# An encoder trunk on one core: the output product takes all 1536 rows in its seven block products, and the fourth weight sum grows in the second's tile

## The chip, the cores and the metric

The kernel runs on one core of one Trainium2 chip. The metric is device microseconds of one execution, given as a median of several runs. Profiles are of one execution. The engines are TensorE (PE, with PEld for its weight loads), VectorE (DVE), ScalarE (ACT), GpSimd (POOL) and SyncE (SP). Each executes its own instructions in program order; semaphores order them against one another.

## The reference

A trunk of two layers on 512 tokens of width 1024, in float32. Each layer normalises its input, projects it (mixer heads, memory query heads, gate), runs eight mixer heads and four heads of cross attention into 256 memory tokens, multiplies the 1536 concatenated head outputs by a SiLU gate, and multiplies by `w_out` onto the residual.

```python
for i in range(DEPTH):                      # 2 layers
    h = rmsnorm(x, norm_g[i])
    mem_h = rmsnorm(mem, mem_norm_g[i])
    ...                                     # layer 0: dilated window attention, layer 1: axial rotary GQA
    o_mem = memory_attention(q_mem, mem_h, w_mem_kv[i], mem_qn_g[i], mem_kn_g[i])
    y = jnp.concatenate([o_mix, o_mem], axis=-1) * jax.nn.silu(gate)   # (1, 512, 1536)
    x = x + jnp.einsum('bse,ed->bsd', y, w_out[i])                     # (1536, 1024)
```

## The kernel before

**Precision.** Every large product is made of three matmuls: both operands are split into a high part (a cast to `float32r`) and a low part (the rest), and high x high, low x high and high x low are accumulated. `mm_early` (L170, L171) issues the two that need the weights' high part, `mm_late` (L174) the one that needs their low part.

**Block products.** Most products are done as 2 x 2 blocks with seven block products instead of eight (Winograd's form of Strassen's method): `s_chunk` goes through `PRODUCTS`. The left factor comes as seven blocks (`12`, `11`, `S1`, `S2`, `S4`, `S3`, `22`), sums and differences of quarters. The right factor's seven blocks come from `Weights`: four quarters from DRAM and the sums `T1 = 12 + 11`, `T2 = T1 + 22` and so on, with signs laid out beforehand. Each finished product is copied (`keep`) or added onto an earlier one (`add`) out of PSUM, and each output block is handed to a consumer `ev`.

**Weights.** An item of weights is a tile of 128 x 1024. It is loaded by SP (L246), possibly summed (`sum`: T1 on DVE at L264 or, from layer B on, by an accumulating DMA from POOL at L260; T2 by a tile-to-tile accumulating DMA, L269; T3 by one from DRAM, L274; T4 by a tile-to-tile one in the tile of block `21`, L279), then split: high part on ACT (L295), low part on DVE (L305), in rings of four. `Weights.advance()` is called once behind every group of matmuls. It issues, in this order, low parts, one sum, high parts and loads; `LEAD` and `ripe` demand a number of groups between a load or sum and what uses it. `KEEP` bounds the raw tiles alive, and `PLAN` lists the chunks: `W2` and `W2b` have two items per block, `W1` and `W1b` one, `T2` and `O1` are plain products.

**Order of the work.** One program order is written out by the host: matmul groups of the projections in sequence, and behind each group `drv.tick()`, in which generators issue their next step: evictions, norms, attention heads (`attn_a` in layer A, `attn_b` in layer B, both "bulk" generators), gates and so on. A generator that waits for another's result yields slots. So attention is spread between the groups of later projections, and a step's place in the order decides what covers it. Where a group needs a block that no generator has made yet, `drv.tick()` is called without a matmul group until it exists.

**The end of a layer.** The gate is projected in three chunks of four heads: memory heads (8 to 11), heads 0 to 3, heads 4 to 7. `gates` multiplies each output block by the heads' output (stored to DRAM by the attention, `od`, and loaded back as `og`). The first two chunks (1024 rows of the product) are turned into seven blocks by `prep_y`. The output product `out_proj` runs `s_chunk` on these 1024 rows: 7 products x 2 items, 14 groups of 12 matmuls of 512 columns. Each output block is added by an accumulating DMA (L876) onto a tile `acc` that was loaded with the residual. The other 512 rows, heads 4 to 7, are the direct part: `gates` splits them into `ys` (L801, L803), and `out_rest` multiplies them plainly, 2 column halves x 4 token blocks, 8 groups of 12 matmuls, added to `acc` by DVE at L756. In layer A the result goes on through norm and transposition into the second layer's first chunks, behind eight groups of the memory projection (`T2b`); in layer B it is written out.

Of the kernel before, what the change touches and what calls it, by code (L numbers as in the profile page):

```python
# [34 lines left out]
PLAN = ["W2"] + ["T2"] * 2 + ["W1", "W2s"] + ["W2" if c.isdigit() else "W1" for c in A_ORDER[1:]] + ["W2"] + ["O1"] * 2 + ["T2b"] * 2 + ["W1bs"] + ["W1b"] * 6 + ["W2b"] + ["O1"] * 2  # L35
# [90 lines left out]
def trunk_kernel(ctx: ExitStack, tc: tile.TileContext, x, mem, wall, norm_g, mem_norm_g, gcol,  # L126
# [57 lines left out]
    GROUPS = {"T2": (2, 2), "T2b": (2, 2), "O1": (1, 4)}  # L184

    def pieces(kind):

        return 2 * GROUPS[kind][0] if kind in GROUPS else 4 if kind in ("W1", "W1b", "W1bs") else 8

    class Weights:  # L190
        def __init__(self):
# [3 lines left out]
            for c in SEQ:  # L195
# [13 lines left out]
                else:  # L209
                    n = 1 if kind in ("W1", "W1b", "W1bs") else 2  # L210
                    at = {k: d + i * n for i, k in enumerate(("21", "11", "12", "22"))}
                    self.allocs += [((c, k, x), at[q] + x, kind) for k, q in LOADS for x in range(n)]
                    for k in ORDER:
                        for x in range(n):
                            self.items.append((c, k, x))
                            self.last.append(g)
                            self.need.append(len(self.items))
                            if k[0] == "T":
                                self.sums.append(((c, k, x), at["11" if k == "T1" else "22"] + x))
# [10 lines left out]
        def use(self, key):  # L230
            if key[1] == "T4":
                key = (key[0], "21", key[2])
# [18 lines left out]
        def sum(self, force=False, want=None):  # L251

            for n, (key, d) in enumerate(self.sums[:8]):
# [110 lines left out]
    def s_chunk(n, act, ev, tokens=True, pre=None, half=False, soon=False):  # L364
# [20 lines left out]
        def add(q, name, u, b):  # L385
# [3 lines left out]
            V.tensor_tensor(t, b, t, ALU.subtract if q == "12" else ALU.add)  # L389
# [4 lines left out]
        for i, (a, s, fresh) in enumerate(PRODUCTS):  # L394
            while a not in act:
                drv.tick()
            if fresh:
                bank[s] = [pj() for _ in range(units)]
            for x in range(units):
                wh, wo = [t.rearrange("p (k c) -> p k c", c=n) for t in W.take()]  # L400
                ah, al = act[a][:, 0], act[a][:, 1]
                def regions():
                    for b in range(2):
                        o = bank[s][b] if units == 2 else bank[s][0][:, b * 256:(b + 1) * 256]
                        for k in range(per):
                            yield b, k, x * per + k, slice(b * 128, (b + 1) * 128), o

                for b, k, kk, bs, o in regions():
# [4 lines left out]
                    st = fresh and kk == 0 and (units == 2 or b == 0)  # L413
# [4 lines left out]
                for b, k, kk, bs, o in regions():  # L418
                    if tokens:
                        mm_late(o, ah[:, kk, bs], wo[:, k], kk == 3)  # L420
                    else:
                        mm_late(o, wo[:, k, bs], ah[:, kk], kk == 3)
                drv.free()
                W.advance()
                if x == units - 1:
# [317 lines left out]
    def out_rest(ys, acc, done, evac):  # L743

        for n in range(2):
            def group(w, u, b, p):
                cs = slice(b * 128, (b + 1) * 128)
                while any(y is None for y in ys):
                    drv.tick()
                for k in range(4):  # L750
                    mm_early(p, ys[k][0][:, cs], w[k][0], ys[k][0][:, cs], w[k][1], k == 0)
                for k in range(4):
                    mm_late(p, ys[k][1][:, cs], w[k][0], k == 3)

            def ev(b, p, n=n):
                V.tensor_tensor(acc[b][n], p, acc[b][n], ALU.add)  # L756
                yield 1
                while (n, b) not in done:
                    yield 1
                yield from evac(n, b, acc[b])  # L760
            chunk(1, 4, group, ev)


    def gates(od, o_done):

        ys, yf, y_done, YW = [None] * 4, [None, None], set(), {}

        def gate(H, first, g, half=False):


            yt = [[m4(F32R, "y").rearrange("p (h t) -> p h t", h=2) for _ in range(2)] for _ in range(2)] if g == 2 else None
# [3 lines left out]
            def ev(q, u, t):  # L775
# [23 lines left out]
                yield 1  # L799
                tv = t.rearrange("p (h t) -> p h t", h=2)  # L800
                A.copy(yt[j][0][:, :, ts], tv)  # L801
                yield 1
                V.tensor_tensor(yt[j][1][:, :, ts], tv, yt[j][0][:, :, ts].bitcast(F32), ALU.subtract)  # L803
                y_done.add((g, i, j))
                if {(2, 0, j), (2, 1, j)} <= y_done:
                    for k in range(2):
                        ys[2 * j + k] = (yt[j][0][:, k], yt[j][1][:, k])
# [51 lines left out]
        return gate, prep_y, YW, ys  # L859

    def out_proj(YW, ys, src, evac, tiles, half=False):

        acc, done = {}, set()

        def load():
# [709 lines left out]
```

## Time and profile before

| | |
|---|---|
| median of 3 runs | 966.77 us (965.88 to 971.68) |
| profiled execution | 968.3 us, its span 966.5 us |
| PE busy | 946.8 us, 98% of the span, 5682 matmuls |
| DVE, ACT, POOL busy | 791.4, 681.7, 341.4 us |
| output product in layer A, first group to the group behind it | 572.83 to 644.09 us |
| output product in layer B, first group to the end of the span | 882.94 to 966.5 us |
| DMA | 209.81 MB, 217 GB/s on average |
| mean granted clock of TensorE | 0.996 |

Times in the rows are microseconds from the start of the span; a row names the engine, the line of the kernel, the operation, and the tiles written and read. Matmul durations in the rows overlap; the distance between starts tells the rate. A bracket at the end gives the idle time of the engine just before, and what ended it.

### The profile page before, as it was taken

The page shows a single profiled execution, that of the slowest core. Times are in us where ns is not written, and L with a number is a line of the kernel's source. Part 1 is how long each engine was busy: PE and PEld are TensorE (multiplying, and loading weights), DVE is VectorE, ACT ScalarE, POOL GpSimd, SP SyncE. Part 2 cuts the span into 40 slices and gives each one's busy share as a digit, 9 for nine tenths or more (in the row PEclk, how much of TensorE's full clock was granted, in tenths as well). Part 3 has the DMA queues.
Part 4 walks back from the last instruction along what each step waited for, and adds up shares of the span by engine and source line. Part 5 has one row for each costly group of instructions (what it writes and reads, how often), then busy time and mean ns, then how long its engine had stood idle before and what let it go on. Part 6 is the DMA issues. An engine that isn't in the chain of part 4 may idle for free.

```text
span 966.5 us, 16604 instructions
## 1 busy us (share of the span) xinstructions
PE 946.8 (98%) x5682; PEld 833.2 (86%) x5682; DVE 791.4 (82%) x1411; ACT 681.7 (71%) x1701; POOL 341.4 (35%) x482
## 2 busy tenths in 40 slices
PE   8999999999999999999999999999899999999998
PEld 5879888888888888888899997788899999998886
DVE  5898676878888888888888999769878898769883
ACT  5775689686868686868685657546768977879770
POOL 1512423557554545454726011322332330111010
PEclk9999999999999999999999999999899999999999
DMA  9989956969686868685959889889766687777744
GB/s 360 317 235 327 271 116 172 294 120 268 149 258 143 262 150 258 154 261 132 283 132 241 266 206 297 268 242 366 167 157 129 199 235 179 207 204 190 206 131 131
DMA packets 89129, 209.81 MB, mean 217 GB/s; under 512 B 25298, under 2 KB 36050, under 8 KB 89044
## 3 DMA queue, kind: packets, MB, share of 16 engines
q1 hardware_dynamic: 69892, 145.76, 43.4%
q0 software_dynamic: 17856, 60.83, 33.4%
q10 hardware_dynamic: 1296, 2.16, 0.6%
q8 instruction: 45, 0.74, 0.3%
q14 instruction: 40, 0.33, 0.1%
HBM read 157.27 MB, written 12.65 MB: 176 GB/s over the span
## 4 chain that ended last, share of the span: by engine, by line
PE 80%; DVE 8%; DMA 6%; ACT 3%; issue 2%; POOL 1%; SPq 0%; DVEq 0%; POOLq 0%; ACTq 0%
PE pj L170 21%; PE pj L171 21%; PE pj L174 20%; DVE wo L305 2%; PE qT L585 2%; PE sa L1106 1%; PE oo L1208 1%; PE pt L1187 1%; PE sa L1102 1%; PE ptb L1405 1%; DMA og<-odb 1%; DMA acc<-sn 1%; DMA wl<-wl 1%; DMA grB<-in_qn_b_dram 1%; DMA od<-o 1%
## 5 line engine op out<-in xcount | busy, mean ns | idle before, releaser
L305 DVE TENSOR_TENSOR wo<-wl,wh 128x1024 fp32r<-128x1024 f32 x255 | 315.1, 1242 | 6.0 <-ACT wh L295 5.8
L295 ACT CAST wh<-wl 128x1024 fp32r<-128x1024 f32 x255 | 268.5, 1060 | 29.3 <-PE pj L171 18.9
L170 PE MATMUL pj<-wh,hS 128*128 128x512 f32 (+1 forms) x448 | 159.0, 368 | 3.9 <-DVE sn L389 3.9
L171 PE MATMUL pj<-wh,hS 128*128 128x512 f32 (+1 forms) x448 | 153.6, 356 | 0.0
L170 PE MATMUL pj<-wh,h 128*128 128x512 f32 (+1 forms) x336 | 117.9, 365 | 0.0
L171 PE MATMUL pj<-wh,h 128*128 128x512 f32 (+1 forms) x336 | 114.0, 353 | 0.0
L437 POOL TENSOR_TENSOR rstd<-mse,half 128x4 f32<-128x4 f32 (+2 forms) x98 | 103.1, 1052 | 8.2
L174 PE MATMUL pj<-wo,hS 128*128 128x512 f32 (+1 forms) x448 | 100.8, 355 | 2.0 <-DVE wo L305 2.0
L170 PEld LDWEIGHTS pj<-wh,hS 128*128 128x128 f32 x448 | 85.9, 192 | 14.8 <-issue 2.6
L171 PEld LDWEIGHTS pj<-wh,hS 128*128 128x128 f32 x448 | 86.1, 192 | 10.3
L372 ACT COPY sn<-pj 128x512 f32<-128x512 f32 x132 | 73.1, 590 | 29.7 <-PE pj L174 29.7
L436 POOL TENSOR_SCALAR mse<-hss 128x4 f32<-128x4 f32 (+1 forms) x86 | 45.1, 525 | 132.2 <-ACT junk L573 128.0
L174 PEld LDWEIGHTS pj<-wo,hS 128*128 128x128 f32 x448 | 75.3, 191 | 14.5 <-DVE wo L305 2.7
L573 ACT ACTIVATE junk<-sn 128x128 f32<-128x128 f32 x264 | 79.1, 308 | 4.1 <-DVE sn L383 4.1
L1050 POOL TENSOR_TENSOR ta<-sn,tabs 128x128 f32<-128x128 f32 (+1 forms) x64 | 37.4, 592 | 118.6 <-DVE sn L578 92.0
L389 DVE TENSOR_TENSOR sn<-pj,sn 128x512 f32<-128x512 f32 x99 | 67.7, 686 | 12.3 <-PE pj L174 11.8
L174 PE MATMUL pj<-wo,h 128*128 128x512 f32 (+1 forms) x336 | 74.8, 352 | 0.0
L171 PEld LDWEIGHTS pj<-wh,h 128*128 128x128 f32 x336 | 63.8, 190 | 7.4
L170 PEld LDWEIGHTS pj<-wh,h 128*128 128x128 f32 x336 | 63.6, 189 | 7.4 <-DVE sn L389 0.2
L279 POOL DMA_DIRECT2D wl<-wl x33 | 29.1, 881 | 111.9 <-DVE wo L305 56.0
L174 PEld LDWEIGHTS pj<-wo,h 128*128 128x128 f32 x336 | 56.0, 189 | 8.7
L578 DVE TENSOR_TENSOR sn<-sn,rstd 128x512 f32<-128x512 f32 (+1 forms) x82 | 48.0, 594 | 7.2 <-POOL rstd L437 7.2
(235 smaller groups left out, 2335.1 us busy)
## 6 DMA issues: line engine op xcount, KB each, us to landing
wl<-in_wall_dram SPq DMA_DIRECT2D x222, 512.0 KB, 7.0
wl<-wl POOLq DMA_DIRECT2D x66, 512.0 KB, 5.5
wl<-in_wall_dram POOLq DMA_DIRECT2D x42, 512.0 KB, 8.5
acc<-sn POOLq DMA_DIRECT2D x16, 256.0 KB, 4.8
od<-o SPq DMA_DIRECT2D x12, 256.0 KB, 5.6
og<-od SPq DMA_DIRECT2D x12, 256.0 KB, 5.5
odb<-o SPq DMA_DIRECT2D x12, 256.0 KB, 3.4
og<-odb SPq DMA_DIRECT2D x12, 256.0 KB, 4.2
```

Source lines behind the costliest of these rows:

```text
L170: T.matmul(o, a, b, start=start, stop=False, skip_group_check=True)
L171: T.matmul(o, c, d, start=False, stop=False, skip_group_check=True)
L174: T.matmul(o, a, b, start=False, stop=stop, skip_group_check=True)
L295: A.copy(wh, self.tile[self.items[i]])
L305: V.tensor_tensor(wo, self.tile[key], wh.bitcast(F32), ALU.subtract)
L372: A.copy(t, b)
L389: V.tensor_tensor(t, b, t, ALU.subtract if q == "12" else ALU.add)
L436: G.tensor_scalar(e, ss, EPS, None, ALU.add)
L437: G.tensor_tensor(r, e, half[:, 0:n], ALU.pow)
L573: A.activation(jk, p[:, j * 128:(j + 1) * 128], AF.Square, scale=QS, accum_out=ss[:, j:j + 1])
L578: V.tensor_tensor(xn[:, 0:n], p.rearrange("p (a b) -> p a b", a=4)[:, 0:n], r[:, 0:n, None].to_broadcast([128, n, 128]), ALU.mult)
L1050: G.tensor_tensor(ta[:, 0:n], xn[:, 0:n, 0:32], ropeA[:, 0, b, s0:s0 + n], ALU.mult)
```

## The change

`out_rest` and the direct part go. Every block product of the output product now takes 768 of the 1536 rows instead of 512: three items and three groups per product (kinds `W3` and `W3b`), 21 groups in all. The first two groups of a product use the blocks of `prep_y` (`YW`), the third uses blocks (`YL`) that a new generator, `prep_l`, makes from the gate's last chunk in the same seven combinations. `gates` therefore stops splitting that chunk and keeps its four blocks in `yl`. A loop in `s_chunk` ticks until the block that the coming group needs exists; it stood ahead of each product and now stands ahead of each group.

The residual is no longer held in `acc`: for three of the four output quarters an accumulating DMA adds it onto a kept product (`Base.add`), for the fourth DVE adds the product onto a loaded tile (`Base.tile`). The consumers `ev_o` and `ev_o2` get each output block once, final.

The fourth weight sum, in all chunks: T4 is now made in T2's tile, by adding the block `21` from DRAM, once T2's own low part is done; before, it was made in block `21`'s tile by adding T2's tile.

```diff
-PLAN = [...] + ["W2"] + ["O1"] * 2 + ["T2b"] * 2 + ["W1bs"] + ["W1b"] * 6 + ["W2b"] + ["O1"] * 2
+PLAN = [...] + ["W3"] + ["T2b"] * 2 + ["W1bs"] + ["W1b"] * 6 + ["W3b"]
-T1_DMA = 17
+T1_DMA = 16
-KEEP = {"T2": 8, "T2b": 6, "O1": 6, "W1": 9, "W2": 10, "W2s": 9, "W1bs": 9, "W1b": 7, "W2b": 9}
+KEEP = {"T2": 8, "T2b": 6, "W3": 11, "W3b": 9, "W1": 9, "W2": 10, "W2s": 9, "W1bs": 9, "W1b": 7}
...
                             if k != "T4":
-                                self.users[c, k, x] = 1 if k in ("22", "T3") or k == "11" and c >= T1_DMA else 2
+                                self.users[c, k, x] = 1 if k in ("21", "22", "T3") or k == "11" and c >= T1_DMA else 2
...
-                    if not (self.ripe(self.lo_at, (c, "21", x), force, 1) and self.ripe(self.at, (c, "T2", x), force)):
+                    if not self.ripe(self.lo_at, (c, "T2", x), force, 1):
                         continue
-                    self.tile[key] = self.tile[c, "21", x]
-                    G.dma_start(self.tile[key], self.tile[c, "T2", x], accum_op=ALU.add)
-                    self.use((c, "T2", x))
+                    self.tile[key] = self.tile[c, "T2", x]
+                    G.dma_start(self.tile[key], wall[d], accum_op=ALU.add)
...
         def keep(name, u, b):
+            if base and name == "s3":
+                t = snap[name, u] = base.tile(u)
+                V.tensor_tensor(t, b, t, ALU.add)
+                c = snap[u, "22"] = snap["s5", u]
+                V.tensor_tensor(c, c, b, ALU.subtract)
+                yield 1
+                yield from ev("22", u, c)
+                return
             t = snap[name, u] = s2(name="sn")
-            A.copy(t, b)
+            A.activation(t, b, AF.Copy, scale=-1.0 if base and name == "s2" else 1.0)
             yield 1
+            if base:
+                base.add(name, u, t)
...
         for i, (a, s, fresh) in enumerate(PRODUCTS):
-            while a not in act:
-                drv.tick()
             if fresh:
                 bank[s] = [pj() for _ in range(units)]
-            for x in range(units):
+            groups = units if more is None else 3
+            for x in range(groups):
                 wh, wo = [t.rearrange("p (k c) -> p k c", c=n) for t in W.take()]
-                ah, al = act[a][:, 0], act[a][:, 1]
+                src = act if x < units else more
+                while a not in src:
+                    drv.tick()
+                ah, al = src[a][:, 0], src[a][:, 1]
...
-                V.tensor_tensor(t, t, o, ALU.mult)
-                yield 1
-                tv = t.rearrange("p (h t) -> p h t", h=2)
-                A.copy(yt[j][0][:, :, ts], tv)
-                yield 1
-                V.tensor_tensor(yt[j][1][:, :, ts], tv, yt[j][0][:, :, ts].bitcast(F32), ALU.subtract)
+                V.tensor_tensor(t, t, o, ALU.mult)
+                yl[i, j] = t
...
+        def prep_l():
+            def put(k, src):
+                t = m4(F32R, "yl")
+                A.copy(t[:, 0:512], src)
+                V.tensor_tensor(t[:, 512:1024], src, t[:, 0:512].bitcast(F32), ALU.subtract)
+                YL[k] = t.rearrange("p (a k t) -> p a k t", a=2, k=2)
...
+            yield from wait((0, 0))
+            put("11", yl[0, 0])
+            yield from wait((0, 1))
+            put("12", yl[0, 1])
+            yield from wait((1, 1), (1, 0))
...
+            put("S1", s1)               # then S2, S4, S3 and 22, a sum ahead of each
...
+    class Base:
...
+        def add(self, name, u, t):
+            G.dma_start(t, self.part(*{"z": (0, 0), "s2": (0, 1), "s5": (1, 1)}[name], u), accum_op=ALU.add)
...
-        drv.spawn(load(), ACC_AT)
-        s_chunk(512, YW, ev, half=half)
-        out_rest(ys, acc, done, evac)
+        drv.spawn(base.load(), ACC_AT)
+        s_chunk(512, YW, ev, half=half, more=YL, base=base)
```

More of the change, by code (lines that the diff above doesn't have):

```diff
@@ L741, in mem_attn @@
                             (0, top, 1), (1, recip, 1), (3, hi, 1), (3, lo, 1), (4, out_, 1), step=step)
[L743 to L756, printed above, removed]
-                yield 1
-                while (n, b) not in done:
-                    yield 1
-                yield from evac(n, b, acc[b])
-            chunk(1, 4, group, ev)
     def gates(od, o_done):
-        ys, yf, y_done, YW = [None] * 4, [None, None], set(), {}
+        yf, yl, y_done, YW, YL = [None, None], {}, set(), {}, {}
         def gate(H, first, g, half=False):
-            yt = [[m4(F32R, "y").rearrange("p (h t) -> p h t", h=2) for _ in range(2)] for _ in range(2)] if g == 2 else None
             if g < 2:
```

142 lines of the change are left out of this document (83 added, 59 removed).

## The prediction

> **What bounds the kernel now.** I read the page first, then the instructions in order of time around the two output products, one engine at a time, then groups and windows of those stretches.
>
> ```profile
> span 966.5 us, 16604 instructions
> PE 946.8 (98%) x5682; PEld 833.2 (86%) x5682; DVE 791.4 (82%) x1411; ACT 681.7 (71%) x1701; POOL 341.4 (35%) x482
> PE 80%; DVE 8%; DMA 6%; ACT 3%; issue 2%; POOL 1%; SPq 0%; DVEq 0%; POOLq 0%; ACTq 0%
> ```
>
> TensorE (PE) is busy almost always and makes up 80% of the chain that ended last. A change pays by the PE instructions it takes out, and costs wherever PE, which executes in program order, meets an instruction whose data are late. Today the output product covers the end of each layer's attention. Layer A (start, duration, engine, line):
>
> ```profile
> 575.58 0.39 PE L170 MATMUL pj<-wh,y 128*128 128x512 f32 x1
> 578.30 0.39 PE L170 MATMUL pj<-wh,y 128*128 128x512 f32 x1
> 644.09 0.39 PE L170 MATMUL pj<-wh,act 128*128 128x512 f32 x1
> ...
> 577.06 1.29 DVE L843 TENSOR_TENSOR ys<-ys,yf 128x512 f32<-128x512 f32 x2
> 579.46 0.16 DVE L1149 TENSOR_TENSOR nmM<-stp,oth 128x8 f32<-128x8 f32 x1
> 608.18 0.69 DVE L1220 TENSOR_TENSOR o<-oo,o 128x512 f32<-128x512 f32 x1 [1.30 <-PE oo L166]
> 618.25 1.38 DVE L798 TENSOR_TENSOR sn<-sn,og 128x512 f32<-128x512 f32 x2 [1.84 <-DMA og<-od]
> ```
>
> The first two rows start the second and third groups of the output product; a group is 12 matmuls of 512 columns: 2.72 us, 0.227 us a matmul. The third row starts the first group behind the product's 22. When the third group starts, the last head has not yet combined its softmax sums (nmM, 579.46); its output is complete at 608.87, and stored, reloaded and gated at 619.6. PE runs block products meanwhile, because the last part of the gated heads, `ys`, is first read in `out_rest`. Layer B is alike:
>
> ```profile
> 882.94 0.48 PE L170 MATMUL pj<-wh,y 128*128 128x512 f32 x1
> 891.13 0.39 PE L164 MATMUL sb<-kbT,qb 128*128 128x512 f32 x1
> 931.98 0.64 PE L174 MATMUL ob<-pbT,vb 128*128 128x256 f32 x4
> 933.05 0.33 SPq L1295 DMA_DIRECT2D odb<-o  x1
> 937.72 1.37 DVE L798 TENSOR_TENSOR sn<-sn,og 128x512 f32<-128x512 f32 x2 [2.48 <-DMA og<-odb]
> 961.50 1.07 PE L174 MATMUL pj<-wh,y 128*128 128x512 f32 x4
> ```
>
> Its product starts at 882.94; the attention steps behind the second group run from 891.13 to 932.6, spread between groups; the gated values exist at 939.1. The last matmul ends at 962.57, 3.9 us before the span does.
>
> **The change part by part.** *Matmuls.* Per layer `out_rest` loses 2 x 4 x 12 = 96; the seven products gain 7 x 12 = 84. That is 12 x 0.227 = 2.7 us less per layer, 5.4 in all; 21 groups stand where 22 stood.
>
> *The moved need.* Each product now has three groups, the third on `YL`, which `prep_l` makes from the gate's last block. Its first reader is the third group of the first product, on `YL["12"]`, and that needs the last heads of the layer. While it is missing, `s_chunk` calls `drv.tick()` with no matmuls between. The compared instruction orders show it: in layer A all of the last head's remaining PE work (16 transposes, 8 and 12 matmuls) stands between the second and the third group, where before it was spread behind groups 6 to 10; in layer B ten attention steps stand there, where before they stood one by one. This term decides: what was covered is in the open, with store, reload, gating and splitting behind it. Behind the waiting matmul stand all 19 later groups; on the other engines only the evictions of the first product wait for it. On SP the gap holds the last loads of gate and residual but no weight loads, since `W.advance()` runs by groups; so the sums on POOL keep their lead in groups.
>
> Layer A, from 578.4 (end of the second group). VectorE (DVE) has done L843 at 578.3 before; one more first weight sum (1.2 us) and one split less put it at about 580.0 after gating. From there to the last head's combine it has 37 instructions in order: 20 that are 512 wide (block sums and low parts of y, gating, splits), one weight low part, 8 scalings, 8 small ones.
>
> ```profile
> L305 DVE TENSOR_TENSOR wo<-wl,wh 128x1024 fp32r<-128x1024 f32 x15 | 18.3, 1223 | 1.7 <-ACT wh L295 1.7
> L823 DVE TENSOR_TENSOR yS<-yf,yS 128x512 fp32r<-128x512 f32 x4 | 2.6, 690 | 0.0
> L1174 DVE TENSOR_SCALAR p<-p,c 128x256 f32<-128x256 f32 x6 | 1.8, 351 | 0.0
> 608.90 0.33 SPq L1002 DMA_DIRECT2D od<-o  x1
> ```
>
> Back to back they overlap by 0.09: 20 x 0.60 + 1.13 + 8 x 0.27 + about 1.2 = 16.5 us. Waits for ScalarE's high parts and PE's 12 matmuls add some 2.7 and the combine 0.6: 599.8. Store to gating took 618.25 - 608.90 = 9.35; both multiplies 1.3 and the low part 0.7 make it 611.2, where PE goes on. Bounds: 604 (no waits, and 937.72 - 933.05 = 4.7 from store to gating as in layer B), and 621 (every step at its old pace: 619.6 + 1.4).
>
> *The clock after a gap.*
>
> ```profile
> 685.25 0.55 PE L170 MATMUL pj<-wh,hS 128*128 128x256 f32 x1 [2.47 <-DVE sn L389]
> 690.34 0.28 PE L170 MATMUL pj<-wh,hS 128*128 128x256 f32 x1
> 693.22 0.28 PE L170 MATMUL pj<-wh,hS 128*128 128x256 f32 x1
> ...
> 686.00:688.00 2.00, 2.00 (x12) 2.00 (x11) 2.00 (x4) 1.20 (x9) 0.70 (x1) 0.50 0.00 0
> 681.56 1.22 PE L174 MATMUL pj<-wo,hS 128*128 128x256 f32 x8 [1.81 <-DVE wo L305]
> ```
>
> After two short waits (1.81 and 2.47 us) the granted clock, third column from the right, was 0.50, and a group took 5.1 us instead of 2.9. I add the same 2.4 us (with the slow first matmul) behind each new gap; bounds 0 and, were the clock halved throughout, the rival below. The Trainium skill ("TensorE: Matmul & The Clock Gate", Part 1) says that the clock halves after an idle window of about 3.4 us and returns after about 3.4 us of work; by it the price would be an estimated 1.7 us a gap. The row disagrees in part, since neither wait was 3.4 us long; the measurement decides.
>
> Then 19 groups, 51.7 us, and 16 transposes of memory tokens that stand among them, 2.0:
>
> ```profile
> L488 PE MATMUL xT<-ident,m 128*128 128x128 f32 x16 | 2.3, 276 | 0.8 <-issue 0.7
> ```
>
> 611.2 + 2.4 + 51.7 + 2.0 = 667.3 against 644.1: layer A loses 23.2 us. DVE doesn't bound the 19 groups: 19 low parts and some 34 other instructions, 45 us.
>
> Layer B: the first two groups keep their times; the burst starts at 891.1.
>
> ```profile
> L1396 ACT ACTIVATE pb<-pb,rdb 128x512 f32<-128x512 f32 x9 | 6.6, 731 | 0.6 <-DVE rdb L1392 0.4
> L1409 ACT CAST pbT<-ptb 128x512 fp32r<-128x512 f32 x10 | 5.8, 585 | 6.4 <-PE ptb L1405 6.4
> L1385 DVE TENSOR_REDUCE nmb<-sb 128x1 f32<-128x512 f32 x8 | 5.5, 688 | 0.5 <-PE sb L166 0.5
> L1414 DVE TENSOR_TENSOR pbT<-ptb,pbT 128x512 fp32r<-128x512 f32 x11 | 7.5, 681 | 1.3 <-ACT pbT L1409 1.3
> 909.94 0.69 DVE L798 TENSOR_TENSOR sn<-sn,og 128x512 f32<-128x512 f32 x1 [3.42 <-DMA og<-odb]
> ```
>
> By the order, DVE has about 21 us of work in the burst, ScalarE (ACT) 21, PE 15. Least is 21; most is the old pace, 932.6 - 891.1 = 41.5. I take ACT's 21 with its old waits for transposes (6.4) and one wait for a reload (3.4): 30, nearer the engines' own sums because the low parts of weights, 17 us of DVE in that stretch before, are gone from it. The last `ob` ends at 921.1; 939.1 - 932.6 = 6.5 to gated values, 0.8 to split: 928.4. With 2.4 + 51.7 the matmuls end at 982.5. The tail is 3.9 as before and 0.6, since both last blocks are now added behind the last group: 987.0, 20.5 us later.
>
> *The weight sums.* T4 now grows in T2's tile from DRAM, behind T2's low part.
>
> ```profile
> wl<-wl POOLq DMA_DIRECT2D x66, 512.0 KB, 5.5
> wl<-in_wall_dram POOLq DMA_DIRECT2D x42, 512.0 KB, 8.5
> acc<-sn POOLq DMA_DIRECT2D x16, 256.0 KB, 4.8
> L295 ACT CAST wh<-wl 128x1024 fp32r<-128x1024 f32 x255 | 268.5, 1060 | 29.3 <-PE pj L171 18.9
> ```
>
> From issue to landing a sum from DRAM takes 8.5 us instead of 5.5, which the orders leave room for: in wide blocks the sum is issued three groups or more before its high part. In ten narrow blocks the order puts its high and low parts one to two groups later, the low part just ahead of its group, where before the next block's first low part stood:
>
> ```profile
> 776.24 1.22 DVE L305 TENSOR_TENSOR wo<-wl,wh 128x1024 fp32r<-128x1024 f32 x1
> 777.38 1.12 PE L174 MATMUL pj<-wo,h 128*128 128x256 f32 x8
> 878.45 1.22 DVE L305 TENSOR_TENSOR wo<-wl,wh 128x1024 fp32r<-128x1024 f32 x1
> 880.93 1.12 PE L174 MATMUL pj<-h,wo 128*128 128x256 f32 x8
> ```
>
> The first two rows are the tightest such place: the low part ended 0.1 us behind the start of the next late matmuls. In the other pair 1.26 us were to spare, and elsewhere that or more. I take 0; at worst ten times 1.2, which reaches into the range's upper part. Three more weight items per layer (3.2 us ACT, 3.7 DVE), three or four more sums on POOL, seven splits of `yl` for four of `y`, the residual in six accumulating DMAs for eight: all lie under the 51.7 us of matmuls. The residual's DMA is a new wait: DVE may not add the next product before it lands. It is issued one group behind the copy it adds to, and the next product's add comes three groups (8.2 us) behind that copy; 8.2 - 2.7 leaves 5.5 for a landing of 4.8. Where it fails, DVE waits about a microsecond, and the low parts behind it are two groups ahead of PE. Tiles freed earlier only start loads earlier, which nothing waits for: 0.
>
> *Sum.* 23.2 + 20.5 = 43.7 (the matmul saving is in it). The profiled execution took 968.3 us for a span of 966.5; it becomes 1012. The median of the runs, 966.77, becomes 1010.5.
>
> **The rivals.** (1) *Half clock through both gaps.* PE's share in layer B's burst is only half, as around 684 us. Its 15 us become 30 in a dependent chain, perhaps 10 more, and 3 more in layer A, with DVE as late as before in places: 1025. Against it: PE is never idle long in layer B's burst. (2) *Relief behind layer A.* Between 644 and 699 PE loses 1.81 + 2.47 + 2.4 = 6.7 us because the second layer's input is late. Two of its four row blocks are now normalised some four groups earlier; if the loss vanishes: 1004. Against it: the other two come a group later than today. (3) *One gap fails to open*, say because layer B's ten steps are bound by less than 21 us and its reload hides: 990. (4) *The other side, not slower:* the last heads land before PE reaches the third group. Then only the matmuls count, 966.8 - 5.4 = 961. It decides from `YL["12"]` ready by 578.3 and 891.3; against it stand nmM at 579.46 and ten steps still to issue. That the change doesn't do what it says is the same case.
>
> **How the numbers follow.** Forecast 0.62; half clock 0.15; relief 0.14; one gap 0.06; the other side 0.03. The likeliest gives 1010.5. All bounds together: layer A from 604 without clock price (13.6) to 621 (33), layer B from 21 (9.1) to 41.5 (32): 989 to 1032. They won't all fall on one side, so 995 to 1030. About 1% is what a measurement of this kernel can tell from no change: slower by more 0.96, within 0.03 (the other side), faster 0.01.
>
> **What would show it.** Right: PE idle some 27 to 33 us between the second and third group of layer A's output product with waits on DVE `yl`; a burst of `sb`, `ptb`, `ob` without `pj` of about 30 us in layer B and 7 us of idle PE behind it; granted clock 0.50 at both restarts; 2.72 us a group afterwards; PE's count lower by 24 matmuls. Wrong: `pj` groups among the last attention steps, or a total below 990, would break the moved need; waits of PE on `wo` in narrow blocks would break the weight-sum term.

## The result and the profile after

The changed kernel takes 1017.5 us (median of 4 runs, 1016.79 to 1018.33) against 966.34 for the kernel before (4 runs, 965.88 to 971.68): a ratio of 1.0512, 95% interval 1.0486 to 1.0539. The prediction was 1010.5, within 995 to 1030. The profiled execution has a span of 1015.3 us, 48.8 more than before. Executions that ran over 15% longer than the others of their kernel (two of six of `t4_tile` below, one of the kernel before) are left out of all times and ratios, and so no trace of `t4_tile` is read.

From the page of the changed kernel: the span, the engines, the granted clock in 40 slices of 25.4 us, and the chain that ended last.

```profile
span 1015.3 us, 16602 instructions
PE 957.9 (94%) x5658; PEld 840.3 (83%) x5658; DVE 804.2 (79%) x1420; ACT 691.6 (68%) x1709; POOL 353.4 (35%) x485
PEclk9999999999999999999999978999999999998699
PE 77%; DVE 10%; DMA 7%; ACT 4%; issue 1%; POOL 0%; SPq 0%; DVEq 0%; ACTq 0%; POOLq 0%
```

PE has its 24 matmuls fewer and is nevertheless 11 us longer busy, which is mostly the lower clock in two places (the 7 and 8, and the 8 and 6). The rest of the loss is idle PE. Now the instructions in order of time around layer A's output product: PE, then DVE, then SP.

```profile
579.21 0.40 PE L170 MATMUL pj<-wh,y 128*128 128x512 f32 x1
583.77 1.07 PE L174 MATMUL pj<-wo,y 128*128 128x512 f32 x4
595.35 2.12 PE L1218 MATMUL pt<-ident,p 128*128 128x128 f32 x8 [10.52 <-DVE p L1205]
612.56 0.80 PE L170 MATMUL pj<-wh,yl 128*128 128x512 f32 x1 [7.05 <-ACT yl L850]
617.74 0.40 PE L170 MATMUL pj<-wh,y 128*128 128x512 f32 x1
669.30 0.48 PE L170 MATMUL pj<-wh,act 128*128 128x512 f32 x1
...
605.62 0.69 DVE L1251 TENSOR_TENSOR o<-oo,o 128x512 f32<-128x512 f32 x1 [1.35 <-PE oo L166]
611.11 0.69 DVE L793 TENSOR_TENSOR sn<-sn,og 128x512 f32<-128x512 f32 x1 [4.79 <-DMA og<-od]
...
606.34 0.33 SPq L1033 DMA_DIRECT2D od<-o  x1
```

The second group's last matmuls end at 584.84 and the third starts at 612.56. Between them PE does the last head: it waits 10.52 us for DVE to scale the scores, transposes, multiplies, and waits 7.05 us for the store, the reload, the gating and the split. Of the 27.7 us it is idle for 19.3. The third group lasts from 612.56 to 617.74, 5.18 us instead of 2.72. Layer B:

```profile
907.02 0.48 PE L170 MATMUL pj<-wh,y 128*128 128x512 f32 x1
915.21 0.39 PE L164 MATMUL sb<-kbT,qb 128*128 128x512 f32 x1
932.27 0.80 PE L164 MATMUL sb<-kbT,qb 128*128 128x512 f32 x1 [3.44 <-DVE pbT L1450]
948.63 1.05 PE L174 MATMUL ob<-pbT,vb 128*128 128x256 f32 x4
956.63 0.80 PE L170 MATMUL pj<-wh,yl 128*128 128x512 f32 x1 [6.94 <-ACT yl L850]
...
930.26 0.69 DVE L793 TENSOR_TENSOR sn<-sn,og 128x512 f32<-128x512 f32 x1 [2.57 <-DMA og<-odb]
955.23 1.38 DVE L793 TENSOR_TENSOR sn<-sn,og 128x512 f32<-128x512 f32 x2 [7.08 <-DMA og<-odb]
```

The ten attention steps run from 915.21 to 949.7 with no output group between them, and 6.9 us later the third group starts. In windows (length, busy time of PE, PEld, DVE, ACT and POOL, then the granted clock, the DMA engines' busy share and GB/s):

```profile
590.00:596.00 6.00, 0.65 (x3) 0.49 (x3) 5.20 (x16) 1.91 (x4) 0.00 (x0) 0.50 0.79 276
925.00:930.00 5.00, 3.48 (x23) 2.77 (x23) 2.58 (x4) 3.75 (x9) 0.00 (x0) 1.00 0.71 210
930.00:935.00 5.00, 2.73 (x9) 2.26 (x10) 4.74 (x10) 2.14 (x5) 0.00 (x0) 0.59 0.00 0
950.00:956.00 6.00, 0.00 (x0) 0.00 (x0) 0.77 (x2) 0.14 (x2) 0.00 (x0) 0.50 0.43 156
```

The third place was not predicted. In the gate chunks, ahead of layer A's product, the changed kernel loses 6.4 us: its product starts at 579.21 instead of 572.83. In order of time, POOL, ACT, DVE, PE:

```profile
510.56 0.95 POOL L284 DMA_DIRECT2D wl<-in_wall_dram  x1
...
519.36 2.00 ACT L299 CAST wh<-wl 128x1024 fp32r<-128x1024 f32 x2 [3.39 <-DMA wl<-in_wall_dram]
533.26 0.22 ACT L1185 ACTIVATE e<-d 128x16 f32<-128x16 f32 x1 [7.54 <-DVE d L1183]
...
521.65 0.35 DVE L1093 TENSOR_SCALAR ks<-qT,gk 128x128 f32<-128x128 f32 x1 [5.71 <-ACT ks L1092]
...
537.74 0.36 PE L170 MATMUL pj<-hS,wh 128*128 128x256 f32 x1 [2.79 <-DVE sn L403]
...
535.00:540.00 5.00, 2.26 (x13) 2.29 (x14) 4.90 (x11) 4.37 (x10) 2.00 (x4) 0.84 0.86 163
```

POOL issues the sum T4 from DRAM at 510.56 (L284). ACT is ready to cast it 5.4 us later, waits 3.39 us for the landing and starts at 519.36, 8.8 us behind the issue. ACT works in order, so the attention's `ks` behind that cast waits too, then DVE, which is late for the rest of the chunk, and in the end PE waits for an eviction (2.79 us) and has a lower clock.

Cut at four instants that each trace has (first group of layer A's product, first group behind it, first group of layer B's product, last matmul), the spans of all profiled kernels are, in us; the runs follow below:

| kernel | to product A | product A | between | product B | tail |
|---|---|---|---|---|---|
| before | 572.8 | 71.3 | 238.9 | 79.6 | 3.9 |
| changed | 579.2 | 90.1 | 237.7 | 104.1 | 4.2 |
| `t4_back` | 573.7 | 90.7 | 236.0 | 102.5 | 4.2 |
| `t4_alone` | 578.8 | 73.0 | 238.0 | 79.4 | 3.9 |
| `a_only` | 579.3 | 90.4 | 238.4 | 79.4 | 3.9 |
| `b_only` | 579.4 | 72.0 | 238.6 | 103.7 | 4.1 |
| `no_heads` | 578.9 | 76.4 | 237.9 | 79.2 | 4.2 |
| `defer` | 578.8 | 89.3 | 237.6 | 99.4 | 4.1 |
| `half_b` | 579.6 | 89.9 | 250.2 | 81.2 | 4.2 |
| `warm` | 578.5 | 91.0 | 238.3 | 101.2 | 4.1 |
| `gate_sb` | 578.3 | 82.7 | 237.1 | 94.7 | 3.9 |
| `closed` | 576.6 | 73.1 | 236.7 | 80.2 | 4.2 |
| `cover_b` | 573.7 | 73.2 | 257.4 | 72.3 | 4.2 |

So the 48.8 us are 6.4 ahead of layer A's product, 18.8 in it, -1.1 between, 24.5 in layer B's and 0.3 in the tail. Each row is one execution, and a stage that is the same in several kernels differs between them: the old product A takes 71.3, 73.0, 72.0 and 73.2 us (before, `t4_alone`, `b_only`, `cover_b`). So a difference of 2 us or less between two rows may be no more than that.

### The profile page after: what moved, and what is told of

Read it like the earlier page. It is cut to its first block, busy times and chain, and to the rows that moved or that the text cites. A ratio compares the mean times of both kernels' runs of the same rounds, so it can differ in the third digit from the quotient of the medians.

```text
span 1015.3 us, 16602 instructions
## 1 busy us (share of the span) xinstructions
PE 957.9 (94%) x5658; PEld 840.3 (83%) x5658; DVE 804.2 (79%) x1420; ACT 691.6 (68%) x1709; POOL 353.4 (35%) x485
## 3 DMA queue, kind: packets, MB, share of 16 engines
q1 hardware_dynamic: 69892, 144.71, 41.5%
## 4 chain that ended last, share of the span: by engine, by line
PE 77%; DVE 10%; DMA 7%; ACT 4%; issue 1%; POOL 0%; SPq 0%; DVEq 0%; ACTq 0%; POOLq 0%
PE pj L171 20%; PE pj L170 20%; PE pj L174 20%; DVE wo L309 3%; PE qT L602 2%; DMA og<-od 2%; PE oo L1239 1%; PE sa L1137 1%; DMA og<-odb 1%; PE sa L1133 1%; PE pt L1218 1%; DMA oth<-ds 1%; PE ptb L1441 1%; DMA wl<-wl 1%; PE xT L505 1%
## 5 line engine op out<-in xcount | busy, mean ns | idle before, releaser
L309 DVE TENSOR_TENSOR wo<-wl,wh 128x1024 fp32r<-128x1024 f32 x261 | 323.3, 1248 | 14.7 <-ACT wh L299 14.5
L299 ACT CAST wh<-wl 128x1024 fp32r<-128x1024 f32 x261 | 272.1, 1054 | 65.4 <-PE pj L171 37.9
L454 POOL TENSOR_TENSOR rstd<-mse,half 128x4 f32<-128x4 f32 (+2 forms) x98 | 106.9, 1091 | 8.2
L384 ACT ACTIVATE sn<-pj 128x512 f32<-128x512 f32 x128 | 72.0, 597 | 39.2 <-PE pj L174 33.9
L1081 POOL TENSOR_TENSOR ta<-sn,tabs 128x128 f32<-128x128 f32 (+1 forms) x64 | 43.9, 686 | 128.1 <-DVE sn L595 82.0
L174 PEld LDWEIGHTS pj<-wo,hS 128*128 128x128 f32 x448 | 75.0, 190 | 12.5 <-DVE wo L309 0.6
L453 POOL TENSOR_SCALAR mse<-hss 128x4 f32<-128x4 f32 (+1 forms) x86 | 42.3, 492 | 115.7 <-ACT junk L590 111.6
L403 DVE TENSOR_TENSOR sn<-pj,sn 128x512 f32<-128x512 f32 x95 | 65.1, 685 | 21.7 <-PE pj L174 15.2
L284 POOL DMA_DIRECT2D wl<-in_wall_dram x35 | 32.2, 921 | 137.9 <-DVE wo L309 64.9
L170 PE MATMUL pj<-hS,wh 128*128 128x256 f32 x192 | 49.6, 295 | 2.8 <-DVE sn L403 2.8
```

Source lines behind the costliest of these rows:

```text
L170: T.matmul(o, a, b, start=start, stop=False, skip_group_check=True)
L174: T.matmul(o, a, b, start=False, stop=stop, skip_group_check=True)
L284: G.dma_start(self.tile[key], wall[d], accum_op=ALU.add)
L299: A.copy(wh, self.tile[self.items[i]])
L309: V.tensor_tensor(wo, self.tile[key], wh.bitcast(F32), ALU.subtract)
L384: A.activation(t, b, AF.Copy, scale=-1.0 if base and name == "s2" else 1.0)
```

## The experiments

Each ratio is to the kernel before on the same chip; 0.01 is 9.7 us. The kernel before took 966.3 to 969.7 us (medians) in the series, so "less" and "slower" are differences of ratios, not of the medians.

**`t4_back`: the fourth weight sum as before, the rest changed.**

```diff
...
-                    if not self.ripe(self.lo_at, (c, "T2", x), force, 1):
...
-                    self.tile[key] = self.tile[c, "T2", x]
-                    G.dma_start(self.tile[key], wall[d], accum_op=ALU.add)
+                    if not (self.ripe(self.lo_at, (c, "21", x), force, 1) and self.ripe(self.at, (c, "T2", x), force)):
+                    self.tile[key] = self.tile[c, "21", x]
+                    G.dma_start(self.tile[key], self.tile[c, "T2", x], accum_op=ALU.add)
...
```

> The changed kernel, with the fourth weight sum made as before (in the tile of block 21, by adding T2's tile). Theory: 6.4 of the 51 us come from this edit alone, because T4 from DRAM is issued by POOL only two groups ahead of its high part in the narrow blocks of the gate chunks and lands after 8.7 us, so ACT waits, and everything queued behind it on ACT. Then this run takes about 1011 us, and the group behind layer A's gate chunks starts 6 us earlier than in the changed kernel. Rival: the delay in the gate chunks has another cause (tiles freed at other times, loads), and T4 costs nothing: 1017.

**`t4_alone`: the reverse edit in the kernel before.**

> The kernel before, with nothing but the fourth weight sum moved into T2's tile from DRAM. Theory: it loses by itself the 6.4 us that the changed kernel had lost before its first output product began: 972 to 973 us, with PE waiting around 525 to 540 us. Rival 1: no cost, 966. Rival 2: the sum costs something only together with the three-item blocks of the output product, which fill the tile pool: 966 here although the run with T4 undone gains.

Measured: `t4_back` 1009.17 us, ratio 1.0418 (1.0390 to 1.0445); `t4_alone` 975.44 us, 1.0063 (1.0038 to 1.0087), which is 6.1 us (3.7 to 8.4). `t4_alone` lands on the theory; `t4_back` is 9.1 us faster than the changed kernel, somewhat more than the 6.4 of the theory. In the table `t4_back` has 5.5 of the 6.4 us back ahead of layer A's product, and `t4_alone` has 6.0 lost there; the rest of `t4_back`'s gain lies in stages that differ by less than 2 us. The waits of ACT, summed over the run, for the kernel before, `t4_alone` and the changed kernel (waiter, what it waits for: total, times, longest):

```profile
ACT wh L295 <- DMA wl<-in_wall_dram: 0.8, 1, 0.8
```
```profile
ACT wh L294 <- DMA wl<-in_wall_dram: 21.8, 16, 4.8
```
```profile
ACT wh L299 <- DMA wl<-in_wall_dram: 22.9, 15, 3.4
```

And `t4_alone` shows the same chain at the same place, ACT's 7.55 us behind a late DVE and then PE:

```profile
518.97 2.00 ACT L294 CAST wh<-wl 128x1024 fp32r<-128x1024 f32 x2 [3.26 <-DMA wl<-in_wall_dram]
532.88 0.22 ACT L1153 ACTIVATE e<-d 128x16 f32<-128x16 f32 x1 [7.55 <-DVE d L1151]
...
537.36 0.35 PE L170 MATMUL pj<-hS,wh 128*128 128x256 f32 x1 [2.80 <-DVE sn L388]
```

Most of ACT's 16 waits cost nothing. The one shown, in the first narrow chunk behind the mixer heads, costs most of it: matched in order with the kernel before, the weights' low parts on DVE are 1.0 us late just ahead of it and 4.8 just behind it (in the changed kernel 1.3 and 5.2), and DVE is busy almost without a break from there to PE's wait.

**`t4_tile`: the new place, but adding a tile instead of DRAM.** Block 21's tile is kept for it.

```diff
...
-                    if not self.ripe(self.lo_at, (c, "T2", x), force, 1):
+                    if not (self.ripe(self.lo_at, (c, "T2", x), force, 1) and self.ripe(self.lo_at, (c, "21", x), force, 1)):
                     self.tile[key] = self.tile[c, "T2", x]
-                    G.dma_start(self.tile[key], wall[d], accum_op=ALU.add)
+                    G.dma_start(self.tile[key], self.tile[c, "21", x], accum_op=ALU.add)
+                    self.use((c, "21", x))
```

> The changed kernel, T4 still made late and in T2's tile, but by adding block 21's tile (kept for it) instead of block 21 from DRAM. It parts the two things that the edit changed. Theory 1, the later place decides (T4 can only start when T2's low part is done, two groups ahead of its own high part): ACT still waits, 1015 to 1018 us. Theory 2, the longer landing decides (8.0 to 8.8 us from DRAM against 5.5 to 6.9 from a tile): the wait of 3.4 us on ACT shrinks by about 2, PE's waits behind it and the lower clock vanish, and as in the kernel with T4 undone the time is 1009 to 1011. Both in part: 1012 to 1014.

Measured: 1028.4 us, ratio 1.0610 (1.0579 to 1.0641), slower than the changed kernel by another 9.5 us and outside all three forecasts. In the instruction orders T4 stands ten groups ahead of its high part in the wide chunks of the heads before the change (four in narrow chunks), and four (two) after it, in `t4_tile` as in the changed kernel. So without DRAM, at the late place, nothing is gained. But the run doesn't part the place from the source: the kept tile can itself hold up loads, and where the extra 9.5 us went isn't settled. Both may count at the wait shown above: the late place left 5.4 us from the issue until ACT was ready, and the landing took 8.8 us; in the kernel before, the same sum was issued at 492.33, from a tile, and landed in 4.5 us.

**`a_only` and `b_only`: the new output product in one layer, the old one with its direct part in the other.**

```diff
-PLAN = [...] + ["W3"] + ["T2b"] * 2 + ["W1bs"] + ["W1b"] * 6 + ["W3b"]
+PLAN = [...] + ["W3"] + ["T2b"] * 2 + ["W1bs"] + ["W1b"] * 6 + ["W2b"] + ["O1"] * 2                  # a_only
+PLAN = [...] + ["W2"] + ["O1"] * 2 + ["T2b"] * 2 + ["W1bs"] + ["W1b"] * 6 + ["W3b"]                  # b_only
...
```

> The change in layer A alone; layer B's output product is the one before, with its direct part (the fourth weight sum is the new one everywhere). Theory, from the two traces: 966.3 + 6.4 for the weight sum + 18.8 for layer A's gap - 1 between the layers = 990 to 991 us. Rival: layer A's delay is partly taken back where the second layer's input was late (6.7 us lost there before), which shows only when layer B does not add its own: 984. Rival 2: the two gaps are not independent, since a later start of layer B leaves its attention in another place: over 995.

> The change in layer B alone; layer A's output product is the one before, with its direct part (the fourth weight sum is the new one everywhere). Theory: 966.3 + 6.4 + 24.7 = 997 us, with the burst of attention steps and the idle PE as long as in the changed kernel (41 us between the second and the third group). Rival: part of layer B's loss was inherited from layer A (tiles, loads): under 993. The losses of the two runs, with that of the weight sum counted once, should add up to 51 us.

Measured: `a_only` 992.73 us, ratio 1.0240 (1.0209 to 1.0271); `b_only` 998.38 us, 1.0296 (1.0260 to 1.0333). The spans add up: 24.9 and 31.3 us over the span before, less the 6.6 of `t4_alone` counted twice, is 49.6; the change has 48.8. The two gaps are independent, and neither is taken back later: "between" stays within 236 and 239 us.

**`no_heads`: the third block without the late heads.**

```diff
-                o = load() if {h0, h0 + 1} <= o_done else None
+                o = load() if g < 2 and {h0, h0 + 1} <= o_done else None
...
-                V.tensor_tensor(t, t, o, ALU.mult)
-                yl[i, j] = t
+                if g == 2:
+                    yl[i, j] = t
+                    return
```

> The changed kernel, with the late data taken away: heads 4 to 7 are left out of the gating, so the last chunk's gate values go into the third block as they are (the attention itself still runs, its last four heads go unused). The third group of the first product then waits for one slot instead of 12 or 13. Theory (the moved need is what costs): 966.3, plus 6 to 9 for the fourth weight sum (the two runs on it), minus 5.4 for 24 matmuls: 967 to 970 us. Rival: the three-item products have a price of their own (more sums, the residual's accumulating DMA between the products): 975 to 985.

Measured: 979.24 us, ratio 1.0122 (1.0101 to 1.0143). Without the late heads 38 of the 51 us are gone (1.0512 to 1.0122): in layer B the whole loss (79.2 against 79.6), in layer A 13.7 of 18.8. The total is the rival's, but not for its reason. What stays in layer A is a wait that the theory left out, the last gate chunk's own way through tanh and split:

```profile
590.30 0.79 PE L170 MATMUL pj<-wh,yl 128*128 128x512 f32 x1 [5.81 <-ACT yl L851]
```

The third group then takes 5.59 us at a granted clock of 0.50; 5.8 + 2.9 less the 2.7 saved is 6.0, and the table shows 5.1.

**`defer`: four groups ahead of the need instead of two.**

```diff
...
+        order = [(i, x) for i in range(7) for x in range(groups)]
+        if more is not None:
+            order[:6] = [(0, 0), (0, 1), (1, 0), (1, 1), (0, 2), (1, 2)]
...
```

> The changed kernel with the first two products of each output product interleaved: the four groups on YW first, then the two on YL, so that the need stands behind four groups instead of two. Theory: in each layer the wait ends at the same time as in the changed kernel, and two groups of 2.72 us more lie in front of it: 10.9 us less, 1006.6. Rival: the bursts are bound by the engines' work between two groups (DVE in layer A, the attention chain in layer B), and with matmuls between the steps they get longer by as much: 1012 to 1017.

Measured: 1011.01 us, ratio 1.0452 (1.0425 to 1.0479), 5.8 us less: half, between the two expectations. Layer B gains 4.7 of 5.4, layer A only 0.8. In layer A the first YL group starts 35.6 us behind the product's start, not 33.4, and behind it PE waits once more, since two products now reach their evictions together:

```profile
614.34 0.80 PE L170 MATMUL pj<-wh,yl 128*128 128x512 f32 x1 [7.18 <-ACT yl L861]
634.98 0.50 PE L170 MATMUL pj<-wh,yS 128*128 128x512 f32 x1 [1.65 <-DVE sn L410]
```

**`half_b`: attention steps moved into layer B's gate chunks.**

```diff
-HALF = {"a": 3, "b": 3, "o": 0}
+HALF = {"m": 2, "a": 2, "b": 2, "o": 0}
```

> The changed kernel with more attention half steps in layer B's gate chunks (every second group of all three chunks instead of every third of two): 6 slots are left to wait for, not 12. Theory: DVE is only 70 per cent busy there, the moved steps lie under matmuls, and each slot of the burst took 34.5 / 12 = 2.9 us: 17 us less, 1000. Rival: the moved steps hold up evictions and low parts in the gate chunks, PE waits there instead, and less than 8 us are gained: over 1009.

Measured: 1006.37 us, ratio 1.0400 (1.0381 to 1.0419), 10.8 us less, between the two expectations. Product B lost 22.9 us and "between" gained 12.5. PE waits 0.6 us in the gate chunks, so most of what came back is the steps' own matmuls and transposes, now in those chunks. Moving a step saves only PE's idle part of it.

**`warm`: matmuls that do nothing in the waits.**

```diff
...
                 while a not in src:
                     drv.tick()
+                    for _ in range(6 if more is not None else 0):
+                        T.matmul(bank[1][0], act[a][:, 0][:, 0, 0:128], wh[:, 0], start=True, stop=True, skip_group_check=True)
```

> The changed kernel with six idle matmuls of 512 columns (1.4 us at full clock) behind every slot of the two waits, written to a bank that the second product overwrites; they change no result. Theory (the clock has a price): the third group takes 2.7 us instead of 5.3 and 5.5, which is 5 us less, and in layer B's burst, where the granted clock was 0.59 to 0.80 from 930 to 950 us, PE's part shrinks by another 2 to 4 us: 1008 to 1012. Rival: the burst is bound by DVE, ACT and DMA, the added matmuls stand in the way of the chain, and only the third groups gain: 1012 to 1019.

Measured: 1013.49 us, ratio 1.0475 (1.0448 to 1.0502), 3.6 us less: just inside the rival's range. In layer A the third group takes 2.72 us instead of 5.18, so the price of the restart is shown to be 2.46, nearly all of it the clock (in the changed kernel the group's second matmul also waits 0.23 us for the low part of `yl`). But it starts 3.3 us later, behind matmuls that stood in the chain's way, and product A gains nothing. Layer B gains 2.9 with its clock at 1.00 from 910 to 955 us; its third group starts 2.5 us earlier and still takes 4.63 us, at a mean clock of 0.68 from 955 to 960 us.

**`gate_sb`: the last two heads gated from their tiles.**

```diff
...
+                    if g == 2 and j == 1:
+                        for h in range(2):
+                            V.tensor_tensor(t[:, h * 256:(h + 1) * 256], t[:, h * 256:(h + 1) * 256], o_kept[h0 + h][:, ts], ALU.mult)
+                        yl[i, j] = t
+                        return
                     o = load()
...
```

> The changed kernel, but the last two heads are gated straight from the attention's tiles instead of being stored and loaded back first (they are still stored). Theory: the way from the last head's output to the first matmul of the third group was 6.3 us in layer A and 6.9 us in layer B, of which about 1.5 to 2 are gating and splitting; 4.5 + 5 us less, 1008. Rival: the waiting slots and DVE's queue set that stretch, not the reload: 1014 to 1017.

Measured: 1001.13 us, ratio 1.0340 (1.0301 to 1.0379), 16.6 us less, more than the theory's 9.5 (the four runs lie between 998.4 and 1004.5; the profiled one took 998.4). DVE and PE in layer A, PE in layer B, then windows of the two third groups, with the columns as above:

```profile
603.89 0.69 DVE L1259 TENSOR_TENSOR o<-oo,o 128x512 f32<-128x512 f32 x1 [1.29 <-PE oo L166]
604.50 1.42 DVE L789 TENSOR_TENSOR sn<-sn,o 128x256 f32<-128x256 f32 x4
...
606.01 0.50 PE L170 MATMUL pj<-wh,yl 128*128 128x512 f32 x1 [2.23 <-ACT yl L855]
606.74 0.50 PE L171 MATMUL pj<-wh,yl 128*128 128x512 f32 x1 [0.22 <-DVE yl L856]
940.20 0.50 PE L170 MATMUL pj<-wh,yl 128*128 128x512 f32 x1 [0.98 <-ACT yl L855]
...
606.00:609.00 3.00, 2.77 (x11) 2.04 (x12) 3.00 (x5) 1.53 (x2) 0.00 (x0) 1.00 0.95 298
940.00:943.00 3.00, 2.58 (x10) 1.90 (x11) 2.91 (x5) 1.71 (x3) 0.00 (x0) 1.00 0.79 254
```

From the last head's combine to the third group it is now 1.4 us instead of 6.3. The rest is the clock: both third groups run at a granted clock of 1.00 and take 3.39 us, not 5.18 and 5.32. What they have above 2.72 is the first two matmuls, the second of which waits for the low part of `yl`. Per layer, the third group starts 5.7 and 7.4 us earlier and is 1.8 and 1.9 us shorter.

**`closed`: `t4_back`, `defer` and `no_heads` together.**

> The three causes taken out together: T4 as before, the third groups behind four groups instead of two, and heads 4 to 7 left out of the gating. No slot is left to wait for. Theory: what remains of the change is the saving of 24 matmuls, 5.4 us, less what the layers' ends lose: 961 to 965 us, faster than before. The run without the heads still waited 5.8 us in layer A for the gate's own last block; two more groups in front take all of it. Rival: the three-item products cost more than they save by themselves: 967 to 972.

Measured: 972.24 us, ratio 1.0035 (1.0015 to 1.0056), still 3.4 us slower than before: the rival. With no slot left to wait for, the saving doesn't appear. Product A is 1.8 us longer than before and product B 0.6, though each has 2.7 us less of matmuls. The waits of PE that remain there, and a wait of DVE ahead of layer A's product:

```profile
540.54 0.69 DVE L805 TENSOR_TENSOR yf<-sn,og 128x512 f32<-128x512 f32 x1 [4.76 <-DMA og<-od]
...
590.13 0.50 PE L170 MATMUL pj<-wh,yl 128*128 128x512 f32 x1 [2.39 <-ACT yl L863]
612.77 0.50 PE L170 MATMUL pj<-wh,yS 128*128 128x512 f32 x1 [2.14 <-DVE sn L411]
...
929.22 1.22 PE L174 MATMUL ob<-pbT,vb 128*128 128x256 f32 x4 [2.71 <-DVE pbT L1463]
```

In layer A, PE waits 4.5 us for ACT and DVE, in layer B 2.7. The first group behind the 2.39 us of waiting takes 4.94 us, most of it at a granted clock of 0.50. Another 3.8 us of this span were lost ahead of layer A's product, where `t4_back`, with the fourth weight sum made the same way, lost 0.9; the reload that DVE waited for came later (4.76 us of waiting against 3.21). Why is not settled. Since the old product A varies by 1.9 us, this run shows that the saving of 2.7 us per product does not appear, and the waits that stand there; it doesn't show a price beyond that.

**`cover_b`: the change in layer B alone, with all that helped.** T4 and layer A as before; in layer B `defer`, `gate_sb` and `HALF = {"a": 1, "b": 1, "o": 0}`.

> The change kept in layer B alone, with everything that the runs before gave for its need: T4 and layer A as in the kernel before; in layer B the third groups behind four groups, the last two heads gated from their tiles, and a half step behind every group of the last two gate chunks, so that no slot is left to wait for. Theory: a moved attention step costs only the PE time that was idle in the burst (in the run with half steps 23 us left the wait, 12.6 came back as matmuls in the gate chunks), so with none left idle layer B keeps most of its 2.7 us of saved matmuls: 964 to 968 us, the same as before or just faster. Rival: DVE is then the bound, through evictions and low parts late at the denser steps, as in the run with three causes taken out, where PE waited 2 to 5 us on DVE at three places: 970 to 976.

Measured: 982.33 us, ratio 1.0153 (1.0133 to 1.0173); both expectations were too low. Product B is 7.3 us shorter than before, but the gate chunks hold the moved steps ("between" is 18.5 us longer, of which PE's waits in the gate chunks are 3.0), and one new wait of 10.12 us stands in the product. PE, DVE, POOL and ACT there:

```profile
942.14 0.80 PE L170 MATMUL pj<-wh,yS 128*128 128x512 f32 x1 [10.12 <-DVE sn L411]
941.40 0.69 DVE L411 TENSOR_TENSOR sn<-pj,sn 128x512 f32<-128x512 f32 x1 [9.94 <-DMA sn<-x1d]
...
926.44 0.86 POOL L291 DMA_DIRECT2D wl<-wl  x1 [6.30 <-DVE wo L317]
929.11 1.77 POOL L954 DMA_DIRECT2D sn<-x1d  x2 [1.80 <-ACT wh L307]
...
940.21 1.04 ACT L307 CAST wh<-wl 128x1024 fp32r<-128x1024 f32 x1 [8.10 <-DMA sn<-x1d]
```

The residual's DMA is issued in two transfers from 929.11 on, behind a weight sum for which POOL had waited 6.3 us, and they land 10.6 and 11.7 us after their issue. DVE's add waits for it, and ACT waits too, with the store of an output block ahead of its casts. No version here beats the kernel before.

## Why the prediction was right, point by point

**The moved need** was right in both layers: `no_heads` takes it away and 38 of 51 us go with it, and `a_only` and `b_only` show each layer's part by itself.

**Layer A** was forecast at +23.2 and cost 18.8. From the second group's end the last head's output was forecast after 21.4 us and took 21.5 (584.84 to 606.31), with DVE's instructions in order as counted. (The 8 matmuls behind the transposes are 16 in both traces; no term used them. PE's last wait is for ACT's high part of `yl`, where the forecast named DVE.) The term that was mis-sized is store to gating: 9.35 taken from the row of before, where 317 GB/s were moved in the same time; now, at 153 GB/s, it took 4.8 (606.34 to 611.11), near the lower bound of 4.7. That the traffic made the difference is likely but not tested. The clock's 2.4 us were 2.46, with the short wait for the low part in it. The 19 groups and 16 transposes came to 54.3 without that, for 53.7.

**Layer B** was forecast at +20.5 and cost 24.7 with the tail. The burst took 34.5 us instead of 30, within the bounds of 21 and 41.5; it started where the forecast had it. Behind it came 6.9 for 7.3 us, 2.6 for 2.4 of clock, and the groups at 2.72. The 4.5 us too few are in the burst's own waits: DVE stood 2.57 us at 930.26 for a reload ahead of the maximum that the next step needed, PE idled 3.44 us behind it, and the clock fell to 0.59. That is the first rival in part. `warm`, at full clock, starts the third group 2.5 us earlier behind the product's start, but this is net of what its added matmuls cost, so the clock's own part in the burst is not shown. The row also bears on the Trainium skill ("TensorE: Matmul & The Clock Gate", Part 1), which has the clock halve after an idle window of about 3.4 us. The traces agree only in part: here the clock was at 0.50 from 930.9, 2.1 us into the idle time, and in the gate chunks PE idled no more than 2.79 us before the clock halved at 538.4.

**The weight sums** were the step that failed. The prediction took 0 for them, with room for a landing of 8.5 us. It gave the lead to wide blocks and weighed in narrow ones only whether the low part came in time on DVE. The high part comes first, on ACT, and there the lead was two groups of 2.9 us for a landing of eight: 6.1 (`t4_alone`) to 9.1 us (`t4_back`) in all. "Waits of PE on `wo` in narrow blocks" would have been the sign; PE's wait was on an eviction two engines further on.

**The residual's DMA** was taken at about 0. In the changed kernel DVE waited 6.2 us for it once, and PE didn't wait there; the landing was 10.1 us in layer A, not 4.8. In `cover_b`, where PE came without a gap, PE waited 10.1 us for the add behind it.

**Relief** behind layer A did not come: PE waits 4.75 us there after the change, against 5.60 before (1.32, 1.81 and 2.47), and "between" is shorter by 1.1. The errors of layer A (-4.4), layer B (+4.2), the sums (+6.4) and "between" (-1.1) make the span 5.1 us longer than forecast. That the first two nearly cancel is luck: one term of layer A was too large, and waits in layer B's burst were left out. The median, 1017.5, is 7 above: the forecast had taken 1.5 us off because the profiled execution of before was that much above its median, and the changed kernel's lies 0.5 below.

## What to carry over

Before an operand is moved to an earlier reader, find the last instruction that makes it and what runs in the meantime: 5.4 us of saved matmuls were set against two gaps of 28 and 41 us that had been covered. Count a sum's lead at its first reader, in groups of the shortest kind, and follow the in-order queue behind that reader, since the stall shows on another engine. Pulling hidden work forward saves only the idle part of it.

## What the runs showed of the hardware

The price of the clock after a gap does not follow from the last wait alone. Read in narrow windows, the granted clock was either 1.00 or 0.50, and the stretches at 0.50 lasted 3.4 us or a multiple of it: 538.4 to 541.8, 589.6 to 603.2 and 610.1 to 616.9 in the changed kernel. A group of 12 matmuls that restarts inside such a stretch, or runs into one, is slow: 5.18 and 5.32 us behind about 7 us of idle PE, 5.59 behind 5.81 (`no_heads`), 4.94 behind 2.39 (`closed`), where the clock fell only after the restart. Behind 2.23 and 0.98 us in `gate_sb` the clock stayed at 1.00. Matmuls in the gap kept it there in layer A (2.72 us), but not for layer B's third group (4.63 us, behind a last wait of 1.53).

An accumulating DMA of 256 KB from DRAM landed in a median of 10.1 us in layer A's product and 5.5 in layer B's:

```profile
sn<-in_x_dram POOLq DMA_DIRECT2D x6, 256.0 KB, 10.1
sn<-x1d POOLq DMA_DIRECT2D x6, 256.0 KB, 5.5
```
